# Seven-product feed-forward on one core: gate and up in turn, sums on VectorE, output weights two blocks at a time

## The chip, the cores and the metric

The kernel runs on one core of a Trainium2 chip. The metric is the device time of one execution in microseconds (us), the median of several runs. A core has TensorE (PE, the matrix engine, with PEld for its weight loads), VectorE (DVE), ScalarE (ACT), GpSimd (POOL) and SyncE (SP, which only issues transfers here). Each engine works through its own list of instructions in order and waits on semaphores for the others. Matrix products gather in PSUM; everything else lies in SBUF.

## The reference

Two trunk layers over 640 tokens (128 of context, 512 latent) of width 1024, with the same weights for both kinds of token. The part that matters here is the feed-forward stage, of which each layer has two:

```python
D_MODEL = 1024
D_FF = 2816
def swiglu(x, wg, wu, wd):
    return (jax.nn.silu(x @ wg) * (x @ wu)) @ wd
def trunk_layer(h, cond, p, ctx):
    ...
    x = rmsnorm(h, p["norm_ffn2"]) * (1 + sc3) + sh3
    h = h + 0.5 * g3 * swiglu(x, p["ffn2_w_gate"], p["ffn2_w_up"], p["ffn2_w_down"])
    return h, new_ctx
```

All of it is in float32. After the second layer only a last normalisation follows.

## The kernel before

**Numbers.** Every float32 operand of a product is held as a high and a low part (`whi`, `wlo` for weights, `xh`, `xl` for the input, `hh`, `hl` for the hidden activation), and a product is three matmuls: high by high, low by high, high by low. The high part is made on ACT (L232), the low part by a subtraction on DVE (L233).

**Tiling.** Activations stand with the model width on the partitions and tokens as columns, in two halves of 256 and 384 columns. The 2816 hidden columns are 22 f blocks of 128. A feed-forward stage goes through chunks of f blocks: the gate and up products of a chunk, SiLU and the product of the two (`hx`), its split into `hh` and `hl`, and then the output phase (`res_phase`), in which 8 output blocks of 128 are summed over the f blocks of the chunk and added to the residual `hT` by DVE (L679).

**The last feed-forward stage.** Only the second layer's second one (`l` 1, `j` 2) uses `CHUNKS_S`, and it is the place of the whole change. Its first chunk is computed plainly: the first two f blocks (the lead group, L754 to L764) by half, each half for both blocks with the inner dimension outermost, other f blocks one at a time through `mm3` (L309 to L311). From `CHUNKS_S[1][0]` on, f blocks go in pairs through `st_pair`, a scheme with 7 block products in place of 8 (Strassen's, in Winograd's form): weights and input are cut in two by two blocks, 128 f columns by 512 of the width, and 512 of the width by 320 tokens. For gate and for up in turn it runs the products named 11, 21, T2, T1, T3, 22 and T4, each 12 matmuls of 320 columns (L852 to L854). Between them ACT copies partial results out of PSUM (`cp`, L859), DVE adds them to the next (`sg`, L867, or `hx`, L874) and multiplies gate and up (L876). `a` and `c` are two halves of one PSUM tile, of which there are two.

**The sums.** T1, T2, T3 and T4 on the input side are sums of input blocks, made once in `st_x`, a generator that is stepped at L763 in the lead group and run out at L796, ahead of the first output phase. It uses DVE and POOL. On the weight side a slab of two f blocks (8 k blocks by 256 columns, 1 MB, tile `raw`) is used in four forms (`W_ST`): A1 as loaded, and S1, S3 and S24, which `st_sums` makes with four instructions on POOL, three of them in place.

**What sets the order.** `wq` lists the weight pieces in the order of use. `prep_to(n)` splits pieces up to number n into slots of a ring (five in this stage), and asks for the next slab (`load_upto`, issued on SP at L208) when one of the three `raw` buffers comes free; `w(ahead)` takes the next piece and prepares some ahead. An output slab holds two output blocks of 128 columns for the f blocks of the chunk, two pieces. The first two output blocks of a seven-product chunk take the f blocks of the first pair early (`early`), beside the second pair. On top of the order in which the code is written, the framework's scheduler arranges the instructions of each engine by a model of their times.

## Time and profile before

| | |
|---|---|
| median of 3 runs | 2614.9 us (2613.13 to 2615.86) |
| profiled execution | 2610.76 us |
| its span in the trace | 2609.0 us |
| PE busy | 2471.4 us, 95% |
| DVE busy | 1656.3 us, 63% |
| ACT busy | 904.7 us, 35% |
| POOL busy | 458.4 us, 18% |
| read from HBM | 254.44 MB |

The share of PE in the span is an average over stages that differ. The last feed-forward stage runs from about 2100 us to 2598 us of the span; what a change there is worth is read from the stretches of that stage: how long PE is busy in each, and which wait ends last. A matmul's own duration is longer than its distance to the next one, since matmuls overlap, so the floor of a stretch is made from distances between starts.

### The profile page before, as it was taken

How to read it: one execution, taken by the hardware profiler on the slowest of the kernel's cores; microseconds unless marked ns; L12 is line 12 of the kernel's file. 1: busy time of each engine (PE TensorE's matmuls, PEld its weight loads, DVE VectorE, ACT ScalarE, POOL GpSimd, SP SyncE). 2: the span in 40 equal slices, each digit the busy share in tenths (PEclk: the TensorE clock that was granted, in tenths of full speed). 3: DMA queues.
4: the chain of work that ended last, by engine and by line, in shares of the span. 5: the costliest groups of instructions: out<-in, count | busy, mean ns of one | idle time of the engine just before them, and what ended most of it. 6: DMA issues, size and time to landing. Idle time of an engine off the chain costs nothing.

```text
span 2609.0 us, 41506 instructions
## 1 busy us (share of the span) xinstructions
PE 2471.4 (95%) x16800; PEld 2314.1 (89%) x16800; DVE 1656.3 (63%) x3308; ACT 904.7 (35%) x1760; POOL 458.4 (18%) x553
## 2 busy tenths in 40 slices
PE   7999999999899999999999999999979968998898
PEld 5999999987679899999999999999756868898888
DVE  5767676665777776454366666656477785555455
ACT  5332222242544332222242122224245444333334
POOL 2210100036002121000011000003510052312220
PEclk8999999999999999999999999999989989999999
DMA  8545454330104345243125444432110211222121
GB/s 291 167 126 166 141 162 145 106 117 24 58 17 126 96 139 178 86 129 107 56 87 156 130 146 138 139 112 92 44 53 19 86 49 53 81 89 73 49 81 57
DMA packets 209223, 272.09 MB, mean 104 GB/s; under 512 B 25672, under 2 KB 176424, under 8 KB 208776
## 3 DMA queue, kind: packets, MB, share of 16 engines
q1 hardware_dynamic: 187016, 191.45, 23.3%
q0 software_dynamic: 22016, 78.00, 10.2%
q8 instruction: 132, 2.16, 0.3%
q14 instruction: 59, 0.48, 0.1%
HBM read 254.44 MB, written 14.97 MB: 103 GB/s over the span
## 4 chain that ended last, share of the span: by engine, by line
PE 82%; DVE 8%; ACT 3%; POOL 3%; DMA 2%; issue 1%; SPq 0%; DVEq 0%; ACTq 0%; POOLq 0%
PE gu L309 11%; PE gu L311 11%; PE gu L310 11%; PE y L309 9%; PE y L310 8%; PE y L311 8%; PE st L852 3%; PE st L853 3%; PE st L854 2%; ACT whi L232 2%; PE O L1771 1%; PE y L1869 1%; DVE wlo L233 1%; PE gu L761 1%; PE gu L759 1%; PE gu L760 1%
## 5 line engine op out<-in xcount | busy, mean ns | idle before, releaser
L232 ACT ACTIVATE whi<-raw 128x1024 fp32r<-128x1024 f32 (+3 forms) x388 | 353.4, 918 | 792.4 <-PE y L310 332.7
L233 DVE TENSOR_TENSOR wlo<-raw,whi 128x1024 fp32r<-128x1024 f32 (+3 forms) x388 | 419.2, 1084 | 293.1 <-ACT whi L232 291.6
L309 PE MATMUL gu<-xh,whi 128*128 128x384 f32 (+1 forms) x1920 | 595.6, 310 | 0.8 <-ACT whi L232 0.8
L310 PE MATMUL gu<-xl,whi 128*128 128x256 f32 (+1 forms) x1920 | 591.5, 308 | 0.0
L311 PE MATMUL gu<-xh,wlo 128*128 128x256 f32 (+1 forms) x1920 | 591.2, 308 | 0.3 <-DVE wlo L233 0.3
L309 PE MATMUL y<-hh,whi 128*128 128x384 f32 (+1 forms) x1328 | 413.9, 313 | 17.7 <-ACT hh L775 17.7
L310 PE MATMUL y<-hl,whi 128*128 128x384 f32 (+1 forms) x1328 | 410.7, 310 | 0.0
L311 PE MATMUL y<-hh,wlo 128*128 128x384 f32 (+1 forms) x1328 | 410.5, 310 | 0.0
L309 PEld LDWEIGHTS gu<-xh,whi 128*128 128x128 f32 x1920 | 360.2, 188 | 11.7 <-issue 10.0
L310 PEld LDWEIGHTS gu<-xl,whi 128*128 128x128 f32 x1920 | 360.9, 188 | 2.6 <-issue 2.4
L311 PEld LDWEIGHTS gu<-xh,wlo 128*128 128x128 f32 x1920 | 360.4, 188 | 1.3 <-issue 0.8
L679 DVE SCALAR_TENSOR_TENSOR hT<-y,G,hT 128x128 f32<-128x128 f32 (+1 forms) x504 | 203.5, 434 | 166.3 <-PE y L311 161.9
L444 DVE SCALAR_TENSOR_TENSOR mvec<-wm,cs,mvec 128x512 f32<-128x512 f32 x420 | 294.3, 744 | 9.9 <-DMA wm<-in_w_mod_dram 9.6
L309 PEld LDWEIGHTS y<-hh,whi 128*128 128x128 f32 x1328 | 252.3, 191 | 25.3 <-ACT hh L775 17.9
L399 POOL DMA_DIRECT2D wm<-in_w_mod_dram x128 | 92.4, 722 | 1037.3 <-DVE mvec L444 794.0
L310 PEld LDWEIGHTS y<-hl,whi 128*128 128x128 f32 x1328 | 252.7, 190 | 0.1
L311 PEld LDWEIGHTS y<-hh,wlo 128*128 128x128 f32 x1328 | 252.5, 190 | 0.4 <-issue 0.4
L852 PE MATMUL st<-xh,whi 128*128 128x320 f32 x320 | 100.7, 316 | 20.1 <-DVE hx L874 8.8
L774 DVE TENSOR_TENSOR hx<-sg,gu 128x256 f32<-128x256 f32 (+1 forms) x136 | 65.5, 482 | 82.4 <-ACT sg L772 82.1
L775 ACT ACTIVATE hh<-hx 128x256 fp32r<-128x256 f32 (+1 forms) x136 | 64.0, 471 | 137.1 <-DVE hx L774 136.8
L772 ACT ACTIVATE sg<-gu 128x256 f32<-128x256 f32 (+1 forms) x136 | 58.2, 430 | 139.3 <-PE gu L311 136.5
L776 DVE TENSOR_TENSOR hl<-hx,hh 128x256 fp32r<-128x256 f32 (+1 forms) x136 | 70.1, 518 | 44.9 <-ACT hh L775 44.8
(392 smaller groups left out, 4404.7 us busy)
## 6 DMA issues: line engine op xcount, KB each, us to landing
wm<-in_w_mod_dram POOLq DMA_DIRECT2D x128, 512.0 KB, 4.2
raw<-in_ffn_w_gate_dram SPq DMA_DIRECT2D x44, 1024.0 KB, 5.4
raw<-in_ffn_w_up_dram SPq DMA_DIRECT2D x44, 1024.0 KB
raw<-in_ffn_w_down_dram SPq DMA_DIRECT2D x36, 512.0 KB, 3.7
raw<-in_ffn_w_down_dram SPq DMA_DIRECT2D x16, 1024.0 KB, 7.5
raw<-in_w_in_dram SPq DMA_DIRECT2D x12, 1024.0 KB, 6.0
raw<-in_ffn_w_down_dram SPq DMA_DIRECT2D x12, 768.0 KB, 5.3
wf<-in_w_mod_dram SPq DMA_DIRECT2D x8, 1024.0 KB, 12.6
```

What stands on the lines that cost most here:

```text
L232: self.nc.scalar.activation(hv, v, AF.Copy)
L233: self.nc.vector.tensor_tensor(lv, v, hv, op=OP.subtract)
L309: self.nc.tensor.matmul(out, wh, xh, start=(i == 0), stop=False)
L310: self.nc.tensor.matmul(out, wh, xl, start=False, stop=False)
L311: self.nc.tensor.matmul(out, wl, xh, start=False, stop=(i == n - 1))
L399: self.nc.gpsimd.dma_start(out=t.rearrange("p (j c) -> p j c", j=2), in_=w[kk * 256:(kk + 1) * 256, c0:c0 + 512].rearrange("(j p) c -> p j ...
L444: nc.vector.scalar_tensor_tensor(self.mvec[:, v], w, c, self.mvec[:, v], op0=OP.mult, op1=OP.add)
L679: self.pin = nc.vector.scalar_tensor_tensor(h, y[:, s:e], G[:, k, v:v + 1], h, op0=OP.mult, op1=OP.add)
L774: nc.vector.tensor_tensor(hx[:, 0:w], sg[:, 0:w], u, op=OP.mult)
L776: self.pin = nc.vector.tensor_tensor(hl[half][:, f, :], hx[:, 0:w], hh[half][:, f, :], op=OP.subtract)
L852: nc.tensor.matmul(o, h, bh[:, k, :], start=start and k == 0, stop=False, skip_group_check=True)
L853: nc.tensor.matmul(o, h, bl[:, k, :], start=False, stop=False, skip_group_check=True)
```

## The change

All of it lies in the last feed-forward stage.

1. `CHUNKS_S` begins with (0, 4), (4, 2) in place of (0, 2), (2, 4): the plain chunk has four f blocks, the first seven-product chunk one pair. There are nine pairs in all, ten before.
2. `st_sums` runs on DVE, and when S1 is split, not when A1 is. `W_ST` becomes A1, S1, S24, S3, and `wq` takes gate and up by turns within each kind. S1's split has tiles of its own, outside the ring.
3. `st_x` runs its sums on DVE alone and makes T1's source a second time in place of keeping it: 60 instructions on DVE, where there were 28 on DVE and 20 on POOL. It is stepped after each product of the plain single f blocks, not in the lead group.
4. `st_pair` runs each of the seven products for gate and then for up, where it ran all seven for gate and then all seven for up. Of the `sg` tiles there are three, not four.
5. Output weights are split two blocks at a time: one piece of 256 columns (`w_down` hands out its halves), and all output blocks of this stage go two at a time. The last `FIN_S` = 6 blocks, 5 before, are run half by half.

```diff
-CHUNKS_S = ((0, 2), (2, 4), (6, 4), (10, 4), (14, 4), (18, 4))
+CHUNKS_S = ((0, 4), (4, 2), (6, 4), (10, 4), (14, 4), (18, 4))
...
-S1_BUFS = 1
-W_ST = ("A1", "S24", "S1", "S3")
+FIN_S = 6
+W_ST = ("A1", "S1", "S24", "S3")
...
+            if f == "S1":
+                hi = self.sx.tile([P, 512], F32R, tag="s1h", name="whi", bufs=2)
+                lo = self.sx.tile([P, 512], F32R, tag="s1l", name="wlo", bufs=2)
+            else:
+                sl = self.i_ring % self.ring_n
+                self.i_ring += 1
+                pool = self.ring_a if sl < RING_A else self.ring_b
+                hi = pool.tile([P, 1024], F32R, tag=f"h{sl}", name="whi")
+                lo = pool.tile([P, 1024], F32R, tag=f"l{sl}", name="wlo")
...
-            if f == "A1":
-                self.st_sums(sid, raw)
...
         if f == "S1":
-            return self.s1.pop(sid)
+            return self.st_sums(raw)
...
-        G = self.nc.gpsimd
+        G = self.nc.vector
...
-        s1 = self.sx.tile([P, 4, P], F32, name="s1", tag="s1", bufs=S1_BUFS)
+        s1 = self.t(512, "s1")[:, 0:512].rearrange("p (k n) -> p k n", k=4)
...
-                            self.add_slab(slab(w, f, 2), W_ST)
+                            self.add_slab(slab(w, f, 2), ())
+                            self.slab_left[len(self.slabs) - 1] = len(W_ST)
+                            if key == "u":
+                                self.wq += [(len(self.slabs) - 2 + i, kind) for kind in W_ST for i in range(2)]
...
-                self.add_slab((src, [P, n, 256]), [(lambda v: v[:, :, 0:P]), (lambda v: v[:, :, P:2 * P])])
+                if st < FB:
+                    self.add_slab((src, [P, n, 256]), [lambda v: v])
+                else:
+                    self.add_slab((src, [P, n, 256]), [(lambda v: v[:, :, 0:P]), (lambda v: v[:, :, P:2 * P])])
...
+    def w_down(self, pairs, ahead):
+
+        if not pairs:
+            return [self.w(ahead)]
+        w = self.w(ahead)
+        return [tuple(v[:, :, i * P:i * P + P] for v in w) for i in range(2)]
...
-                        if half == 1 and k % 2:
-                            next(tprep, None)
...
                         self.mm3(outs[s], [(wh[:, k, :], wl[:, k, :], xh[:, k, :], xl[:, k, :]) for k in range(DB)])
+                        next(tprep, None)
...
-            r12, r11, r22 = whole(V, k, TH), whole(V, k, 0), whole(G, 4 + k, TH)
-            t1 = self.sx.tile([P, TH], F32, name="sg", tag="sg", bufs=4)
-            t1s.append(t1)
-            V.tensor_tensor(t1, r12, r11, op=OP.subtract)
-            G.tensor_tensor(r12, r22, r12, op=OP.subtract)
-            split(G, r12, *(t[:, k, TH:NTOK] for t in self.T23))
-            V.tensor_tensor(r22, r22, t1, op=OP.subtract)
-            split(V, r22, *(t[:, k, 0:TH] for t in self.T23))
-            r21 = whole(G, 4 + k, 0)
-            G.tensor_tensor(r21, r21, r22, op=OP.subtract)
-            split(V, r21, *(t[:, k, :] for t in self.T4))
+            r12, r11, r22 = whole(k, TH), whole(k, 0), whole(4 + k, TH)
+            V.tensor_tensor(r11, r12, r11, op=OP.subtract)
+            V.tensor_tensor(r12, r22, r12, op=OP.subtract)
+            split(r12, *(t[:, k, TH:NTOK] for t in self.T23))
+            yield
+            r21 = whole(4 + k, 0)
+            V.tensor_tensor(r22, r22, r11, op=OP.subtract)
+            V.tensor_tensor(r21, r21, r22, op=OP.subtract)
+            split(r22, *(t[:, k, 0:TH] for t in self.T23))
+            split(r21, *(t[:, k, :] for t in self.T4))
             yield
         for k in range(4):
-            split(V, t1s[k], *(t[:, k, TH:NTOK] for t in self.xt))
+            r12, r11 = whole(k, TH), whole(k, 0)
+            V.tensor_tensor(r12, r12, r11, op=OP.subtract)
+            split(r12, *(t[:, k, TH:NTOK] for t in self.xt))
...
-            g = sg[i, t] = self.sx.tile([P, TH], F32, name="sg", tag="sg", bufs=4)
+            g = sg[i, t] = self.sx.tile([P, TH], F32, name="sg", tag="sg", bufs=3)
...
-        for done in (gate, up):
-            ac = self.d2("st")
-            a, c = ac[:, 0, 0:TH], ac[:, 1, 0:TH]
-            b = self.b([P, 512], name="st")[:, 0:TH]
-            w1 = self.w(2)
-            prod(a, w1, 0, "11", True)
-            t1 = copy(a)
-            prod(b, w1, 4, "21", True)
-            done(0, 0, b, t1)
-            w2 = self.w(2)
-            prod(a, w2, 0, "T2", False)
-            u2 = copy(a)
-            w4 = self.w(2)
-            prod(c, w4, 0, "T1", True)
-            t5 = copy(c)
-            w3 = self.w(2)
-            prod(a, w3, 0, "T3", False)
-            done(1, 1, a, t5)
-            prod(c, w2, 4, "22", False)
-            done(0, 1, c, u2)
-            prod(a, w3, 4, "T4", False)
-            done(1, 0, a, None)
+        B = range(2)
+        done = (gate, up)
+        ac = [self.d2("st") for _ in B]
+        a, c = ([t[:, i, 0:TH] for t in ac] for i in range(2))
+        b = [self.b([P, 512], name="st")[:, 0:TH] for _ in B]
+
+        def pair(o, w, k0, x, start, then):
+            out = []
+            for u in B:
+                prod(o[u], w[u], k0, x, start)
+                out.append(then(u))
+            return out
+
+        w1 = [self.w(2) for _ in B]
+        t1 = pair(a, w1, 0, "11", True, lambda u: copy(a[u]))
+        pair(b, w1, 4, "21", True, lambda u: done[u](0, 0, b[u], t1[u]))
+        w4 = [self.w(1) for _ in B]
+        w2 = [self.w(1) for _ in B]
+        u2 = pair(a, w2, 0, "T2", False, lambda u: copy(a[u]))
+        t5 = pair(c, w4, 0, "T1", True, lambda u: copy(c[u]))
+        w3 = [self.w(0) for _ in B]
+        pair(a, w3, 0, "T3", False, lambda u: done[u](1, 1, a[u], t5[u]))
+        pair(c, w2, 4, "22", False, lambda u: done[u](0, 1, c[u], u2[u]))
+        self.prep_to(self.i_use + 2)
+        pair(a, w3, 4, "T4", False, lambda u: done[u](1, 0, a[u], None))
...
-        first = DB if nxt is None else DB - FIN
+        fin = FIN_S if pairs else FIN
+        first = DB if nxt is None else DB - fin
...
-            wds = [self.w(self.ahead) for _ in range(k)]
+            k = 2 if pairs else lead if db == 0 else 1
+            wds = []
+            while len(wds) < k:
+                wds += self.w_down(pairs, self.ahead)
...
+            one(DB - fin + db, h0, wds[db])
+            self.prep_to(self.i_use + min(db, 1 if pairs else self.ring_n - FIN))
```

The change moves instructions. First VectorE at the end of the first chunk's gate and up. Before, these rows stand ahead of `hx` of f blocks 0 and 1 (L774; `tr`, `t23l` and `t4l` are tiles of `st_x`):

```order
L822 TENSOR_TENSOR t23l_20675<-tr_20768,t23h_20674 128x320 [waits Activation_49]
L831 TENSOR_TENSOR tr_20811<-tr_20811,sg_20813 128x320 [waits Pool_49]
L822 TENSOR_TENSOR t4l_20677<-tr_20778,t4h_20676 128x320 [waits Activation_49]
L822 TENSOR_TENSOR t23l_20675<-tr_20811,t23h_20674 128x320 [waits Activation_49]
L774 TENSOR_TENSOR hx_20828<-sg_20826,gu_20648 128x384 [waits DVE_49,Activation_49]
L774 TENSOR_TENSOR hx_20834<-sg_20832,gu_20649 128x384 [waits DVE_49,Activation_49]
L776 TENSOR_TENSOR hl_20454<-hx_20828,hh_20453 128x384 [waits Activation_49]
L776 TENSOR_TENSOR hl_20454<-hx_20834,hh_20453 128x384 [waits Activation_49]
```

After, the same place (`hx_20750` and `hx_20756` are those of f blocks 0 and 1; `hx` is L787 now, `wlo` L236, the sums of `st_x` L829 and L838):

```order
L787 TENSOR_TENSOR hx_20750<-sg_20748,gu_20650 128x384 [waits Activation_49]
L236 TENSOR_TENSOR wlo_20761<-raw_20459,whi_20760 128x1024 [waits Activation_49]
L236 TENSOR_TENSOR wlo_20765<-raw_20465,whi_20764 128x1024 [waits Activation_49]
L236 TENSOR_TENSOR wlo_20919<-raw_20642,whi_20918 128x1024 [waits DMAHW7_49,Activation_49]
L787 TENSOR_TENSOR hx_20756<-sg_20754,gu_20651 128x384 [waits DVE_49,PE_49,Activation_49]
L829 TENSOR_TENSOR tr_20797<-xh_20345,xl_20346 128x320 [waits DVE_49]
L829 TENSOR_TENSOR tr_20799<-xh_20345,xl_20346 128x320 [waits DVE_49]
L789 TENSOR_TENSOR hl_20454<-hx_20750,hh_20453 128x384 [waits Activation_49]
L829 TENSOR_TENSOR tr_20801<-xh_20345,xl_20346 128x320 [waits DVE_49,Pool_49]
L789 TENSOR_TENSOR hl_20454<-hx_20756,hh_20453 128x384 [waits Activation_49]
L838 TENSOR_TENSOR tr_20799<-tr_20797,tr_20799 128x320 [waits DVE_49]
```

The sums of `st_x` stood ahead of the two `hx`; now three weight splits stand between the two, and the sums follow behind both.

Second, PE near the end of a pair, where product 22 ends and T4 begins, in one PSUM tile. Before, for up (`st_21949`):

```order
L853 MATMUL st_21949<-xl_20346,whi_21901 128x320
L854 MATMUL st_21949<-xh_20345,wlo_21902 128x320
L852 MATMUL st_21949<-xh_20345,whi_21901 128x320
L853 MATMUL st_21949<-xl_20346,whi_21901 128x320
L854 MATMUL st_21949<-xh_20345,wlo_21902 128x320
L852 MATMUL st_21949<-t4h_20676,whi_21986 128x320 [waits DVE_49]
L853 MATMUL st_21949<-t4l_20677,whi_21986 128x320
L854 MATMUL st_21949<-t4h_20676,wlo_21987 128x320
L852 MATMUL st_21949<-t4h_20676,whi_21986 128x320
```

After, for both (`st_22044` is gate, `st_22045` up):

```order
L867 MATMUL st_22045<-xh_20345,wlo_22131 128x320
L865 MATMUL st_22045<-xh_20345,whi_22130 128x320
L866 MATMUL st_22045<-xl_20346,whi_22130 128x320
L867 MATMUL st_22045<-xh_20345,wlo_22131 128x320
L865 MATMUL st_22044<-t4h_20795,whi_22134 128x320 [waits DVE_49]
L866 MATMUL st_22044<-t4l_20796,whi_22134 128x320
L867 MATMUL st_22044<-t4h_20795,wlo_22135 128x320
L865 MATMUL st_22044<-t4h_20795,whi_22134 128x320
L866 MATMUL st_22044<-t4l_20796,whi_22134 128x320
```

T4 followed 22 of the same tile, and T3 stood right ahead of them; now between T3 and T4 of one tile lie three products, one of its own and two of the other.

Third, VectorE at the second pair of a chunk, from the end of the first pair. Before (`raw_21885` is a slab of the second pair, `raw_22013` an output slab):

```order
L876 TENSOR_TENSOR hx_22079<-st_21949,sg_21947 128x320 [waits PE_49]
L233 TENSOR_TENSOR wlo_22137<-raw_21885,whi_22136 128x1024 [waits DMAHW4_49,Activation_49]
L867 TENSOR_TENSOR sg_22115<-st_22084,cp_22101 128x320 [waits Activation_49]
L879 TENSOR_TENSOR hl_21822<-hx_22079,hh_21821 128x320 [waits Activation_49]
L233 TENSOR_TENSOR wlo_22162<-raw_21885,whi_22161 128x1024 [waits Activation_49]
L233 TENSOR_TENSOR wlo_22285<-raw_22013,whi_22284 128x512 [waits DVE_49,DMAHW5_49,PE_49,Activation_49]
L233 TENSOR_TENSOR wlo_22247<-raw_21885,whi_22246 128x1024 [waits PE_49,Activation_49]
L874 TENSOR_TENSOR hx_22241<-st_22210,cp_22227 128x320 [waits DVE_49,Activation_49]
L876 TENSOR_TENSOR hx_22241<-hx_22241,sg_22115 128x320 [waits DVE_49]
L867 TENSOR_TENSOR sg_22177<-st_22083,cp_22159 128x320 [waits PE_49]
L879 TENSOR_TENSOR hl_21822<-hx_22241,hh_21821 128x320 [waits Activation_49]
```

After (`raw_22436` and `raw_22500` are gate's and up's slab of the second pair, `raw_22784` an output slab):

```order
L880 TENSOR_TENSOR sg_22884<-st_22824,cp_22856 128x320 [waits Activation_49]
L236 TENSOR_TENSOR wlo_22841<-s1_22835,whi_22840 128x512 [waits Activation_49]
L259 TENSOR_TENSOR raw_22436<-s1_22826,raw_22436 128x4x128 [waits DVE_49]
L259 TENSOR_TENSOR raw_22500<-s1_22835,raw_22500 128x4x128 [waits DVE_49]
L236 TENSOR_TENSOR wlo_22913<-raw_22436,whi_22912 128x1024 [waits Activation_49]
L236 TENSOR_TENSOR wlo_23041<-raw_22784,whi_23040 128x1024 [waits DMAHW5_49,PE_49,Activation_49]
L887 TENSOR_TENSOR hx_22899<-st_22825,cp_22870 128x320 [waits Activation_49]
L260 TENSOR_TENSOR raw_22436<-raw_22436 128x4x128 [waits DVE_49]
L236 TENSOR_TENSOR wlo_22973<-raw_22500,whi_22972 128x1024 [waits Activation_49]
L260 TENSOR_TENSOR raw_22500<-raw_22500 128x4x128 [waits DVE_49]
L889 TENSOR_TENSOR hx_22899<-hx_22899,sg_22884 128x320 [waits DVE_49,Activation_49]
L236 TENSOR_TENSOR wlo_22905<-raw_22436,whi_22904 128x1024 [waits Activation_49]
```

VectorE had splits and the results of products there; the sums of both slabs (L257 to L260) now stand between them, and the split of an output slab ahead of S24's.

## Rows read from the trace of the kernel before

**Rows 1.** Table by stretches: stretch, length, busy us (instructions) of PE, PEld, DVE, ACT, POOL; clock, DMA share, GB/s

```profile
2099.00:2106.00 7.00, 4.27 (x15) 3.90 (x15) 6.35 (x9) 5.00 (x10) 3.51 (x3) 0.76 0.00 0
2121.00:2139.40 18.40, 0.74 (x8) 0.54 (x6) 18.00 (x26) 6.87 (x17) 13.57 (x15) 0.64 0.23 71
...
2165.00:2253.60 88.60, 80.56 (x530) 77.36 (x529) 48.26 (x77) 31.58 (x52) 22.61 (x16) 1.00 0.23 72
...
2430.70:2519.30 88.60, 80.46 (x529) 77.33 (x528) 49.00 (x76) 31.58 (x52) 22.34 (x16) 1.00 0.23 72
```

**Rows 2.** Timeline of DVE and PE: start, length, engine, line, operation, out<-in, idle before and releaser

```profile
2122.63 1.15 DVE L831 TENSOR_TENSOR tr<-tr,sg 128x320 f32<-128x320 f32 x1
...
2139.40 0.90 PE L309 MATMUL y<-hh,whi 128*128 128x384 f32 x2 [17.66 <-ACT hh L775]
```

**Rows 3.** Waits of PE, 2150 to 2575: waiting line, awaited, us, times, longest

```profile
PE st L852 <- DVE hx L874: 14.7, 20, 1.5
PE st L852 <- ACT cp L859: 13.4, 10, 1.4
PE st L852 <- ACT whi L232: 5.8, 10, 0.6
PE st L852 <- DVE hx L876: 5.5, 5, 1.1
```

**Rows 4.** Timeline of PE: first and last matmul of three runs, and the last output matmul

```profile
2239.77 0.28 PE L311 MATMUL y<-hh,wlo 128*128 128x256 f32 x1
...
2240.84 0.28 PE L311 MATMUL y<-hh,wlo 128*128 128x256 f32 x1
2240.96 0.34 PE L309 MATMUL y<-hh,whi 128*128 128x384 f32 x1
...
2242.88 0.33 PE L311 MATMUL y<-hh,wlo 128*128 128x384 f32 x1
2243.05 0.30 PE L852 MATMUL st<-xh,whi 128*128 128x320 f32 x1
...
2245.98 0.31 PE L854 MATMUL st<-xh,wlo 128*128 128x320 f32 x1
...
2597.82 0.28 PE L311 MATMUL y<-hh,wlo 128*128 128x256 f32 x1
```

**Rows 5.** Timeline of DVE in a seven-product chunk

```profile
2197.69 1.23 DVE L233 TENSOR_TENSOR wlo<-raw,whi 128x1024 fp32r<-128x1024 f32 x1 [0.69 <-ACT whi L232]
2198.84 0.48 DVE L874 TENSOR_TENSOR hx<-st,cp 128x320 f32<-128x320 f32 x1
2199.36 0.49 DVE L876 TENSOR_TENSOR hx<-hx,sg 128x320 f32<-128x320 f32 x1
2200.10 0.49 DVE L867 TENSOR_TENSOR sg<-st,cp 128x320 f32<-128x320 f32 x1 [0.25 <-PE st L854]
2200.51 0.48 DVE L879 TENSOR_TENSOR hl<-hx,hh 128x320 fp32r<-128x320 f32 x1
...
2222.69 0.68 DVE L233 TENSOR_TENSOR wlo<-raw,whi 128x512 fp32r<-128x512 f32 x1
2223.29 0.61 DVE L679 SCALAR_TENSOR_TENSOR hT<-y,G,hT 128x384 f32<-128x384 f32 x1
```

**Rows 6.** Groups by line and shape, 2150 to 2575: busy us, mean ns, idle before

```profile
L233 DVE TENSOR_TENSOR wlo<-raw,whi 128x1024 fp32r<-128x1024 f32 x60 | 82.2, 1369 | 76.4 <-ACT whi L232 76.2
L232 ACT ACTIVATE whi<-raw 128x1024 fp32r<-128x1024 f32 x59 | 62.5, 1060 | 111.5 <-POOL raw L259 44.5 <-PE y L310 33.5 <-PE st L853 32.9
```

**Rows 7.** Timeline of PE around the lead group's second half

```profile
2100.93 0.45 PE L759 MATMUL gu<-xh,whi 128*128 128x384 f32 x1 [1.88 <-ACT xh L639]
...
2102.40 0.69 PE L761 MATMUL gu<-xl,whi 128*128 128x384 f32 x1 [0.85 <-DVE xl L640]
...
2120.70 0.34 PE L761 MATMUL gu<-xl,whi 128*128 128x384 f32 x1
```

**Rows 8.** Page's part on DMA issues: KB each, median us from issue to landing

```profile
raw<-in_ffn_w_gate_dram SPq DMA_DIRECT2D x44, 1024.0 KB, 5.4
```

More of the change, by code (lines that the diff above doesn't have):

```diff
@@ L217, in prep_to @@
             if f in W_ST:
-                v = self.st_view(sid, raw, f)
+                v = self.st_view(raw, f)
             else:
@@ L221, in prep_to @@
             k, w = v.shape[1], v.shape[2]
-            sl = self.i_ring % self.ring_n
-            self.i_ring += 1
-            pool = self.ring_a if sl < RING_A else self.ring_b
-            hi = pool.tile([P, 1024], F32R, tag=f"h{sl}", name="whi")
-            lo = pool.tile([P, 1024], F32R, tag=f"l{sl}", name="wlo")
+            if f == "S1":
[7 more added lines that the diff above has]
+                lo = pool.tile([P, 1024], F32R, tag=f"l{sl}", name="wlo")
             hv = hi[:, 0:k * w].rearrange("p (k n) -> p k n", k=k)
@@ L241, in prep_to, with st_view, st_sums @@
             self.i_prep += 1
[L243 removed]
+    def st_view(self, raw, f):
         if f == "S1":
[L246 removed]
+            return self.st_sums(raw)
         return raw[:, :, P:2 * P] if f == "S3" else raw[:, :, 0:P]
[L249 to L252 removed]
+    def st_sums(self, raw):
+        G = self.nc.vector
         a11, a12 = raw[:, 0:4, 0:P], raw[:, 4:8, 0:P]
         a21, a22 = raw[:, 0:4, P:2 * P], raw[:, 4:8, P:2 * P]
[L255 removed]
+        s1 = self.t(512, "s1")[:, 0:512].rearrange("p (k n) -> p k n", k=4)
         G.tensor_tensor(s1, a21, a22, op=OP.add)
@@ L799, in ffn @@
             self.res_phase(n, [(hh[i], hl[i]) for i in range(2)], [(f, f) for f in range(n)], (l, j), nxt if last else None,
-                           early=(n - 2 if c0 >= st else 0))
+                           early=(n - 2 if c0 >= st else 0), pairs=st < FB)
         if st < FB:
@@ L1840, in out1, with res_phase @@
                 yield
-    def res_phase(self, n, xs, order, G, nxt, lead=1, early=0):
+    def res_phase(self, n, xs, order, G, nxt, lead=1, early=0, pairs=False):
         nc = self.nc
@@ L1859, in res_phase @@
         if early:
-            wds = [self.w(1) for _ in range(2)]
+            wds = self.w_down(pairs, 1)
             ys = [(i, half, self.b([P, 512], name="y")) for i in range(2) for half in range(2)]
@@ L1885, in res_phase @@
             return
-        wds = [self.w(0) for _ in range(FIN)]
+        wds = []
+        while len(wds) < fin:
+            wds += self.w_down(pairs, 0)
         h0, h1 = (1, 0) if nxt[1] is None else (0, 1)
-        for db in range(FIN):
-            one(DB - FIN + db, h0, wds[db])
-            self.prep_to(self.i_use + min(db, self.ring_n - FIN))
+        for db in range(fin):
+            one(DB - fin + db, h0, wds[db])
+            self.prep_to(self.i_use + min(db, 1 if pairs else self.ring_n - FIN))
         self.x = [None, None]
@@ L1893, in res_phase @@
         self.fine = True
-        for db in range(FIN):
-            one(DB - FIN + db, h1, wds[db])
+        for db in range(fin):
+            one(DB - fin + db, h1, wds[db])
         self.fine = False
```

17 lines of the change are left out of this document (6 added, 11 removed).

## The prediction

> **What bounds the kernel now.** The profiled execution took 2610.76 us (span 2609.0 and 1.76 around it), 4.1 under the median of 2614.9, so what the sum saves is taken off the median. The order of work is unchanged until 2098, where the last feed-forward stage begins, so everything below lies there. TensorE (PE) is the limit whenever it is fed, and I read first what it waits for. The table by stretches shows PE busy 0.74 of 18.40 us up to 2139.4, at a granted clock of 0.64 [rows 1]. The wait itself: one product of the output phase stands 17.66 us for a hidden activation `hh` [rows 2]. The four full chunks repeat every 88.6 us [rows 1]. The waits of PE there are on a copy out of PSUM, on `hx` and on weight splits, and sum to 39.4 us over five chunks [rows 3], about 8 a chunk.
>
> Pitches make the floor. Nine starts of 256-column matmuls take 1.07 us (0.119 each), eleven of 384 take 1.92 (0.1745), twenty of 320 take 2.93 (0.1465) [rows 4]. One product of 12 is 1.76 us. A pair of f blocks in seven products (168 matmuls) is 24.6, in the plain form 96 x (0.119 + 0.1745) = 28.2, and the output phase costs 24 x 0.2935 = 7.04 per f block. A chunk of two pairs is 49.2 + 28.2 = 77.4, so 11.2 of 88.6 are lost: about 8 in ten waits, and some 0.3 per wait to get going again. From 2121, where the stretch of the long wait begins [rows 1], to the last output product (2597.8, [rows 4]) are 477 us, of which 10 x 24.6 + 22 x 7.04 = 401 are floor.
>
> **One pair fewer in seven products.** Nine instead of ten: +28.2 - 24.6 = +3.6 us.
>
> **The end of the 17.66 us wait.** Before, 28 instructions of `st_x` on VectorE (DVE) and 20 on GpSimd (POOL) lie ahead of the two `hx` that PE waits for. DVE is busy 18.00 of 18.40 us in that stretch, POOL 13.57 [rows 1], and an instruction of 320 columns that takes 0.48 in the chunks [rows 5] takes 1.15 here [rows 2]. After, 60 such instructions run on DVE with POOL idle, spread over the plain f blocks 2 and 3. Their pitch is 0.41 where the next needs nothing and 0.52 where it does [rows 5]; I take 0.45.
>
> The long splits on DVE, which lie beside GpSimd's sums in the chunks, take 1.37 on average and 1.23 where GpSimd is still; the short sums beside GpSimd's share of `st_x` took 1.15 against 0.48 [rows 2, 5, 6]. So the rows show a loss of a tenth in one place and of a half in the other, and it is the second, with POOL idle after, that 0.45 rests on. The Trainium skill (SBUF: State Buffer, Who interferes with whom) states that a VectorE instruction with two inputs in SBUF and a GpSimd instruction that reads SBUF take turns at a shared port, each for its whole length. By that rule the 60 sums cost the same 60 x 0.45 = 27 us once GpSimd is idle, and 60 x 1.15 = 69 if they had to share; by the rows alone the two numbers are the same.
>
> Start of the stage: PE stands 1.88 and then 0.85 us for `xh` and `xl` [rows 7], and the clock of that stretch is 0.76 [rows 1]. In the new order the first 24 matmuls of f block 2 (2.8 us) lie in this gap. The group still starts when `xl` is there, 2102.4, but at full clock. A clock of 0.76 over 7 us is some 3 us at half of it, ten matmuls of 384 columns, each about 0.15 us dearer than its pitch; so the group ends 1.5 earlier than 2120.9, where its last matmul hands over before [rows 7]: at 2119.4. Then a new wait: the up weights of f block 2 need a ring slot that this group holds, so 1.06 on ScalarE (ACT) and 1.23 on DVE follow [rows 5, 6], with the restart 2.7 us. The rest of blocks 2 and 3 is 25.4: the output phase begins at 2147.5. On DVE four long splits x 1.15, two products of 384 columns x 0.61 and 1.06 on ACT ahead of them end 6.9 after 2119.4 [rows 5, 6]; then 61 short instructions (47 of `st_x`) x 0.45 and four splits x 1.15 = 32, so the last `hl` of the chunk is there at 2158.3. PE has 80 matmuls (11.7 us) ahead of it in the order, to 2159.2. I charge 1 us. The phase ends at 2147.5 + 28.2 + 1 = 2176.7. The T1 parts and the sums for the first pair (21 us of DVE) fit behind that phase and the two double products before T2.
>
> **Gate and up in turn.** Each copy, `sg` and `hx` now has 1.76 us or more of the other product over it, against 0.4 to 0.5 an instruction. The waits on `cp` (13.4) and `hx` (14.7 + 5.5) [rows 3] go. What is late next is the weights.
>
> **Sums on DVE.** Eight of 512 columns per pair at 0.60 [rows 5], 4.8 us; by the duration, 0.68, it would be 5.4. Per pair DVE has 6 splits x 1.15 + 2 x 0.60 + 4.8 + 14 short x 0.45 = 19.2 of PE's 24.6. Enough on average; the queue decides. For a chunk's first pair the weights are made under the output phase before, and nothing waits. For the second pair the order puts the sums behind the last `hx` of the first. Count from the end of T4 of up, t = 0, on DVE: mult 0.5, two sums 1.7, `hl` 2.1, two sums 3.3, S1 3.9, `sg` 4.3, S1 4.9, two sums 6.1, S3 7.3, output weights 8.4, `hx` 8.8, sum 9.4, S3 10.6, sum 11.2, mult 11.6, S24 of gate 12.8, of up 14.0. PE has 11 of both (3.5), then 6 early output matmuls that need ACT's `whi` at 4.95, 20 more that need the 8.5 above, then T2, whose `whi` of up is there at 12.4: waits of 1.4, 2.7 and 0.9, in all 5.0, with restarts 5.9. Four chunks have such a pair: 23.6 us. Of this, 1.15 each is the output split, now 1024 columns (ACT 1.06) in place of 512, that stands ahead of S24; elsewhere that edit is hidden under the output phase.
>
> **Loads.** SP issues the next pair's gate slab once the second output slab is split, 3 us before t = 0 of the second pair, and a slab of 1 MB lands 5.4 us after its issue [rows 8], so at 2.4. `s1` waits for it at the head of DVE's queue, with the last `hl` behind it, and so does ACT's `whi`. For PE about 2.3 us and restarts, 3.4, at three chunk ends, 2.6 at the short chunk, 1.6 at the last. Fewer `sg` buffers and the six last output blocks cost nothing that a row shows; the 11 us behind the last product stay.
>
> **Sum.** 2176.7; short chunk 24.6 + 14.1 + 2.6 = 41.3, to 2218.0; four chunks 4 x 77.4 = 309.6 and 23.6 + 10.2 + 1.6 = 35.4, to 2563.0. Before it was 2597.9: 34.9 us less. On the median 2614.9 - 34.9 = 2580.0.
>
> **Rivals.**
> A, DVE is not late. If the second pair's weights come in time, 23.6 us more go: 2556. For it: DVE is far from full in a chunk, 48 of 88.6 us [rows 1]. Against: the sums stand behind `hx` in an in-order queue. Chance 0.17.
>
> B, the waits are dearer. Gaps of 1.88 and 0.85 us are followed by a clock of 0.76 over that stretch [rows 1, 7], where ten matmuls cost 1.5 us more (as above); eight such places give 12, and sums at 0.68 add 0.6 to each second pair: 2594. Chance 0.23. The Trainium skill (Perfetto Trace Analysis, Optimizing Scalar/DVE Operations) warns that moving work between GpSimd and VectorE might not help; no row of before has the sums on VectorE alone.
>
> C, slower: the loads become the bound. Two of three slab buffers are held by gate and up until S3 and S24 are split. If every pair waits for a full landing and split, 5.4 + 1.06 + 1.23 = 7.7 [rows 5, 6, 8], nine pairs cost 69: 2649. The side turns at 34.9 / 9 = 3.9 us per pair. Against: the second pair's up slab is asked for when S3 of gate is split, ten us before its first use. Chance 0.06.
>
> D, the order is new but the gain is eaten elsewhere, within 0.2%: 0.04.
>
> **How the numbers follow.** The forecast has 0.50. Its own spread is about 8 us. The range takes in A and B and leaves out C, D and the outer tails: 2553 to 2602. A measurement here tells 0.2% (5 us) from no change. Faster 0.90, same 0.04, slower 0.06.
>
> **What would show it.** After: no wait over 3 us in the output phase of the first chunk, and full clock there. Chunks of 84 to 87 us with waits on `wlo` and `whi` at the early output products and T2 of the second pair, none on `cp`. DVE's short instructions at 0.48 throughout, POOL idle. Chunks of 80 would mean A, matmuls at half pitch behind the gaps B, waits on `raw` of several us in every pair C. A first output phase that still stands for `hh` would make the forecast wrong.

## The result and the profile after

The changed kernel takes 2579.16 us in the median of four runs (2577.18 to 2583.58); the kernel before took 2614.98 beside it. The ratio is 0.9866, with a 95% interval of 0.9849 to 0.9883. The profiled execution took 2577.18 us, its span is 2575.4. The part ahead of the last feed-forward stage takes the same instructions in all but the same order in every kernel here, and yet it ends anywhere from 2097.8 to 2107.7 us in their profiled executions; so stages are compared within a trace, and whole kernels by medians.

The page after, first the busy times:

```profile
PE 2466.1 (96%) x16824; PEld 2316.6 (90%) x16824; DVE 1662.7 (65%) x3378; ACT 893.1 (35%) x1726; POOL 324.5 (13%) x453
...
HBM read 254.44 MB, written 14.97 MB: 105 GB/s over the span
```

VectorE's share hardly moved: it took over GpSimd's sums, and its instructions are no longer stretched by GpSimd. The table by stretches after (stretch, length, busy us of PE, PEld, DVE, ACT, POOL, clock, DMA share, GB/s), to be read against [rows 1]:

```profile
2099.00:2106.00 7.00, 6.61 (x42) 5.57 (x41) 6.14 (x9) 4.76 (x10) 3.29 (x3) 1.00 0.00 0
2121.00:2146.50 25.50, 24.97 (x166) 24.97 (x167) 24.17 (x48) 12.82 (x23) 0.00 (x0) 1.00 0.48 152
2146.50:2220.80 74.30, 73.38 (x494) 72.07 (x493) 61.76 (x127) 26.43 (x44) 0.00 (x0) 1.00 0.18 55
2248.76:2335.11 86.35, 80.70 (x528) 78.89 (x528) 52.41 (x89) 30.61 (x49) 0.00 (x0) 0.98 0.23 74
2335.11:2423.34 88.23, 81.89 (x528) 80.09 (x528) 52.51 (x89) 30.61 (x49) 0.00 (x0) 0.96 0.23 72
2423.34:2509.45 86.11, 80.59 (x528) 78.81 (x529) 52.32 (x89) 30.60 (x49) 0.00 (x0) 0.98 0.23 74
2509.45:2565.50 56.05, 52.74 (x342) 51.65 (x342) 36.42 (x72) 24.26 (x45) 1.14 (x1) 0.94 0.11 38
```

The first three rows are the gain: where PE stood 17.66 us at a clock of 0.64, it is now busy in 25 of 25.5 and in 73.4 of 74.3 us, at full clock, while VectorE alone carries the sums (24.17 of 25.50 busy) and POOL does nothing. The full chunks, three of which run from early wait to early wait here, take 86.1 to 88.2 us, against 88.6 before: little was won there, and the clock is no longer 1.00. The waits of PE from 2095 to 2570 say why (awaited, us in total, times, longest):

```profile
PE y L1886 <- DVE wlo L236: 10.2, 4, 2.6
PE y L1886 <- ACT whi L235: 5.5, 4, 1.4
PE st L865 <- ACT whi L235: 3.1, 5, 0.9
PE y L1886 <- DVE hl L892: 3.0, 4, 0.8
```

Nothing is left of the waits on `cp` and `hx` [rows 3]; the two large rows now are weight splits that come late, at the early output products (L1886), in each of the four second pairs. PE's timeline at one of them (start, length, line, operation, idle before):

```profile
2335.11 0.39 PE L1886 MATMUL y<-hh,whi 128*128 128x256 f32 x1 [1.38 <-ACT whi L235]
...
2335.93 0.28 PE L1886 MATMUL y<-hl,whi 128*128 128x256 f32 x1
2338.76 0.58 PE L1886 MATMUL y<-hh,wlo 128*128 128x256 f32 x1 [2.55 <-DVE wlo L236]
...
2343.20 0.52 PE L1886 MATMUL y<-hl,whi 128*128 128x384 f32 x1
2343.51 0.52 PE L1886 MATMUL y<-hh,wlo 128*128 128x384 f32 x1
...
2345.25 0.31 PE L865 MATMUL st<-t23h,whi 128*128 128x320 f32 x1
2345.40 0.31 PE L866 MATMUL st<-t23l,whi 128*128 128x320 f32 x1
```

PE idles 1.38 us, runs six matmuls, idles 2.55 us, and what follows starts every 0.31 us for 384 columns, near twice the 0.1745 of [rows 4]: the lower of the two clock levels, 1.2 GHz, until about 2344.9. The same two waits stand in all four second pairs, and the clocks of the table (0.98, 0.96, 0.98, 0.94) come to some 3.4, 7, 3.4 and 6.7 us at 1.2 GHz behind them. VectorE's timeline just ahead of it:

```profile
2330.33 0.49 DVE L889 TENSOR_TENSOR hx<-st,sg 128x320 f32<-128x320 f32 x1 [2.90 <-PE st L867]
2330.74 1.28 DVE L257 TENSOR_TENSOR s<-raw 128x512 f32<-128x512 f32 x2
2331.94 0.48 DVE L892 TENSOR_TENSOR hl<-hx,hh 128x320 fp32r<-128x320 f32 x1
...
2335.15 1.29 DVE L259 TENSOR_TENSOR raw<-s,raw 128x512 f32<-128x512 f32 x2
2336.35 2.35 DVE L236 TENSOR_TENSOR wlo<-raw,whi 128x1024 fp32r<-128x1024 f32 x2
```

VectorE stands idle for 2.90 us until PE ends T4 of up, and only then begins the sums for the next pair, which stand behind that `hx` in its queue. The second half of the last row is the output split that PE awaits at 2338.76.

### The profile page after: what moved, and what is told of

It is laid out like the page before. It is cut to its first block, busy times and chain, and to the rows that moved or that the text cites. A ratio compares the mean times of both kernels' runs of the same rounds, so it can differ in the third digit from the quotient of the medians.

```text
span 2575.4 us, 41416 instructions
## 1 busy us (share of the span) xinstructions
PE 2466.1 (96%) x16824; PEld 2316.6 (90%) x16824; DVE 1662.7 (65%) x3378; ACT 893.1 (35%) x1726; POOL 324.5 (13%) x453
## 3 DMA queue, kind: packets, MB, share of 16 engines
q0 software_dynamic: 22016, 78.00, 10.3%
## 4 chain that ended last, share of the span: by engine, by line
PE 83%; DVE 9%; DMA 3%; POOL 2%; ACT 2%; issue 1%; SPq 0%; DVEq 0%; ACTq 0%; POOLq 0%
PE gu L310 11%; PE gu L312 11%; PE gu L311 11%; PE y L310 9%; PE y L311 8%; PE y L312 8%; PE st L865 2%; PE st L866 2%; PE st L867 2%; DVE wlo L236 1%; PE O L1787 1%; PE gu L775 1%; PE gu L773 1%; PE gu L774 1%; PE pj L1227 1%; PE y L1886 1%
## 5 line engine op out<-in xcount | busy, mean ns | idle before, releaser
L310 PE MATMUL gu<-xh,whi 128*128 128x256 f32 (+1 forms) x1984 | 616.0, 310 | 0.8 <-ACT whi L235 0.8
L312 PE MATMUL gu<-xh,wlo 128*128 128x256 f32 (+1 forms) x1984 | 611.3, 308 | 0.9 <-DVE wlo L236 0.9
L311 PE MATMUL gu<-xl,whi 128*128 128x256 f32 (+1 forms) x1984 | 611.5, 308 | 0.0
L235 ACT ACTIVATE whi<-raw 128x1024 fp32r<-128x1024 f32 (+2 forms) x362 | 347.0, 964 | 757.8 <-PE y L311 340.1
L236 DVE TENSOR_TENSOR wlo<-raw,whi 128x1024 fp32r<-128x1024 f32 (+2 forms) x362 | 399.1, 1107 | 218.1 <-ACT whi L235 215.1
L310 PE MATMUL y<-hh,whi 128*128 128x256 f32 (+1 forms) x1344 | 417.0, 312 | 0.4 <-DVE hT L680 0.3
L311 PE MATMUL y<-hl,whi 128*128 128x256 f32 (+1 forms) x1344 | 414.7, 309 | 0.6 <-DVE hl L892 0.6
L312 PE MATMUL y<-hh,wlo 128*128 128x256 f32 (+1 forms) x1344 | 414.6, 309 | 0.0
L310 PEld LDWEIGHTS gu<-xh,whi 128*128 128x128 f32 x1984 | 372.5, 188 | 11.9 <-issue 10.0
L311 PEld LDWEIGHTS gu<-xl,whi 128*128 128x128 f32 x1984 | 373.2, 188 | 2.7 <-issue 2.4
L787 DVE TENSOR_TENSOR hx<-sg,gu 128x256 f32<-128x256 f32 (+1 forms) x140 | 67.7, 484 | 81.2 <-ACT sg L785 81.1
L595 POOL TENSOR_TENSOR rst<-ms,mhalf 128x2 f32<-128x2 f32 (+1 forms) x12 | 11.5, 956 | 836.2 <-DVE ms L594 836.2
```

Source lines behind the costliest of these rows:

```text
L235: self.nc.scalar.activation(hv, v, AF.Copy)
L236: self.nc.vector.tensor_tensor(lv, v, hv, op=OP.subtract)
L310: self.nc.tensor.matmul(out, wh, xh, start=(i == 0), stop=False)
L311: self.nc.tensor.matmul(out, wh, xl, start=False, stop=False)
L312: self.nc.tensor.matmul(out, wl, xh, start=False, stop=(i == n - 1))
L787: nc.vector.tensor_tensor(hx[:, 0:w], sg[:, 0:w], u, op=OP.mult)
```

## The experiments

All start from the changed kernel and change what their diff shows. Medians are of four runs each, beside seven of the kernel before on the same chip (2614.9 to 2615.4). The table gives the full chunks that were read from each trace: length, PE's waits in one of them and the clock. Not tried apart from the rest are the pair count, the six last output blocks, the three `sg` tiles and the new order of the four forms.

| kernel | median us | ratio to before, 95% | a full chunk | waits of PE in it | clock |
|---|---|---|---|---|---|
| before | 2615.0 | | 88.6 | 7.9 (39.4 / 5) | 1.00 |
| changed | 2579.2 | 0.9849 to 0.9883 | 86.1 to 88.2 | 6.4 in the longest | 0.96 to 0.98 |
| e1_serial | 2595.6 | 0.9911 to 0.9940 | 89.2 | 7.7 | 1.00 |
| e2_pool_sums | 2574.0 | 0.9827 to 0.9860 | 83.2 to 85.7 | 4.4 | 0.96 to 1.00 |
| e3_stx_pool | 2584.8 | 0.9867 to 0.9907 | 86.4 | 5.8 | 0.98 |
| e4_single_out | 2578.0 | 0.9837 to 0.9870 | 85.5 to 85.9 | 4.5 | 0.96 |
| e5_first_two | 2604.6 | 0.9940 to 0.9973 | 86.4 | 5.8 | 0.98 |
| e6_early4 | 2567.6 | 0.9802 to 0.9836 | 82.7 to 82.8 | 3.1 | 1.00 |
| e8_early22 | 2576.2 | 0.9834 to 0.9863 | 85.4 | 5.1 | 0.98 |
| e10_early4_single | 2557.5 | 0.9759 to 0.9790 | 80.1 to 80.2 | 1.6 | 1.00 |
| e12_early4_single_pool | 2566.7 | 0.9801 to 0.9831 | 82.7 | 4.2 | 1.00 |
| e13_early5_single | 2558.0 | 0.9769 to 0.9802 | 80.1 | 1.5 | 1.00 |
| e14_no_sums | 2561.0 | 0.9780 to 0.9809 | 82.0 | 2.4 | 0.98 |

### Undoing one part at a time

**e1_serial** undoes the alternation of gate and up, in the products and in the order of the weight pieces.

```diff
-        w1 = [self.w(2) for _ in B]
-        t1 = pair(a, w1, 0, "11", True, lambda u: copy(a[u]))
...
+        for done in (gate, up):
+            w1 = self.w(2)
+            prod(a, w1, 0, "11", True)
+            t1 = copy(a)
...
```

> The changed kernel with one part undone: a pair runs all seven products for gate and then all seven for up, as before, and the weight pieces are queued slab by slab; sums on VectorE, chunks and output weights stay new. Theory (the alternation hides the copies and hx): waits of TensorE on cp and hx come back, some 7 us a chunk of two pairs and half that in the short one, in all 4.5 x 7 = 32, less what the waits on late weights in the second pair (5.4 a chunk) ease because the weights of up are needed later: 2590 to 2612. Rival (the weights are the limit either way, so the alternation hides nothing that would show): 2575 to 2586.

Measured: 2595.6, 16.4 above the changed kernel. The theory holds. Waits of PE in two chunks of e1_serial:

```profile
PE st L862 <- DVE sg L877: 6.1, 8, 1.0
PE st L862 <- DVE hx L884: 4.8, 8, 0.7
PE st L862 <- ACT cp L869: 4.4, 8, 0.6
```

They are the waits of before, on copies and on their sums, 7.7 us a chunk, and the early waits on weights are gone. Note the clock: these 24 waits of up to 1 us leave it at 1.00, while fewer and longer ones in the changed kernel do not.

**e5_first_two** gives the first chunk two plain blocks again.

```diff
-CHUNKS_S = ((0, 4), (4, 2), (6, 4), (10, 4), (14, 4), (18, 4))
+CHUNKS_S = ((0, 2), (2, 4), (6, 4), (10, 4), (14, 4), (18, 4))
...
+                        if half == 1 and k % 2:
+                            next(tprep, None)
+                            next(tprep, None)
```

> The changed kernel with the first chunk back at two plain f blocks, ten pairs in seven products, and the x sums stepped in the lead group again (all 60 on VectorE). Theory (the two plain blocks are the cover for the x sums): 60 x 0.45 = 27 us of VectorE and the splits behind it face 20 us of the lead group, so TensorE waits for hh some 8 to 15 us again and runs at half clock behind that, less 3.6 for the pair that is again in seven products: 2583 to 2598. Rival (the sums on VectorE alone are quick enough without cover): 2573 to 2578.

Measured: 2604.6, 25.5 above the changed kernel and 6.6 above the top of what was expected. A wait of 12.46 us is back, in the expected size; it stands at a product of the first pair, on `t4h` of the x sums, and not at the output phase (timeline of PE, then the stretches around it):

```profile
2140.15 0.60 PE L868 MATMUL st<-xh,whi 128*128 128x320 f32 x1 [12.46 <-ACT t4h L836]
```

```profile
2126.00:2140.15 14.15, 1.70 (x14) 1.52 (x13) 13.61 (x32) 6.76 (x15) 0.00 (x0) 0.73 0.68 221
2140.15:2150.00 9.85, 9.85 (x47) 9.85 (x48) 9.85 (x26) 4.08 (x8) 0.00 (x0) 0.69 0.02 4
```

VectorE is busy in 13.61 of 14.15 us with POOL idle: one engine without cover still leaves PE idle for 12.46 us, where two that hinder each other left it idle for 17.66. The expectation left out two things. The chunk (2, 4) then has a second pair of its own, the fifth, with the waits and the clock of such a pair; and PE's waits of 1.88 and 0.85 us at the start of the stage [rows 7] are back too, since no matmuls of f block 2 fill them. So the 25.5 us are the price of all of this together, and not of the place of the sums alone.

**e3_stx_pool** shares the x sums with GpSimd in the new place.

```diff
-            r12, r11, r22 = whole(k, TH), whole(k, 0), whole(4 + k, TH)
-            V.tensor_tensor(r11, r12, r11, op=OP.subtract)
-            V.tensor_tensor(r12, r22, r12, op=OP.subtract)
+            r12, r11, r22 = whole(V, k, TH), whole(V, k, 0), whole(G, 4 + k, TH)
+            V.tensor_tensor(r11, r12, r11, op=OP.subtract)
+            G.tensor_tensor(r12, r22, r12, op=OP.subtract)
...
```

> The changed kernel with the x sums shared between the engines as before (40 on VectorE, 20 on GpSimd), in the new places beside the plain f blocks 2 and 3. Theory (both the engine and the cover matter, the cover more): the 40 on VectorE go from 0.45 to about 1.15 beside GpSimd, 46 us against 27, so the last hl of the first chunk comes some 15 us later and the first output phase or the first pair waits 3 to 12 us: 2582 to 2594. Rival 1 (the place alone did it, the engine is free to choose): 2576 to 2582. Rival 2 (one engine alone was the mistake, sharing helps here): under 2575.

Measured: 2584.8, 5.6 above the changed kernel, the lower part of the theory's range. One group of the x sums on VectorE (busy us, mean ns), in the kernel before from 2121 to 2139.4, then from 2121 to 2160 in e3_stx_pool and in the changed kernel:

```profile
L817 DVE TENSOR_TENSOR tr<-xh,xl 128x320 f32<-128x320 f32 x4 | 3.3, 818 | 0.0
```

```profile
L829 DVE TENSOR_TENSOR tr<-xh,xl 128x320 f32<-128x320 f32 x12 | 9.1, 788 | 0.0
```

```profile
L829 DVE TENSOR_TENSOR tr<-xh,xl 128x320 f32<-128x320 f32 x22 | 10.4, 488 | 0.0
```

Fewer sums on VectorE take nearly as long, 788 ns each against 488. PE then waits 2.13 us for `hl` in the first output phase and 1.28 for `whi` in the first pair. So the engine is worth some 5 us here; the slowest run of the changed kernel (2583.6) is still above the fastest of this one (2581.7), and it is the two waits in the trace that bear the reading out.

**e2_pool_sums** puts the weight sums back on GpSimd.

```diff
-        G = self.nc.vector
+        G = self.nc.gpsimd
```

> The changed kernel with the weight sums back on GpSimd, all else new. Theory (the second pair waits because its sums stand in VectorE's queue behind the last hx): the sums can start earlier but take 1.3 to 1.6 each on GpSimd, eight in a row some 12 us against 11.6 on VectorE after the same point, and the long splits on VectorE go back from 1.23 to about 1.37: 2572 to 2592, and the waits move from the early output products to T2. Rival 1 (VectorE's load alone made the weights late): 2555 to 2568. Rival 2 (the two engines hinder each other so much that sums on GpSimd cost more in all): over 2595.

Measured: 2574.0, 5.2 *below* the changed kernel. That is in the theory's range, but the shift of the waits that went with it did not come: they stay at the early output products, 1.05 and 1.90 in place of 1.38 and 2.55. GpSimd's four kinds of sum take 1.44 to 1.75 us each on average, and the splits of S1 beside them on VectorE go from 683 ns to 1402 (2200 to 2550, the changed kernel first):

```profile
L236 DVE TENSOR_TENSOR wlo<-s,whi 128x512 fp32r<-128x512 f32 x16 | 10.9, 683 | 0.0
```

```profile
L236 DVE TENSOR_TENSOR wlo<-s,whi 128x512 fp32r<-128x512 f32 x16 | 22.4, 1402 | 0.0
```

What stands in VectorE's queue at the start of the second pair is 4.8 us shorter, though (eight sums at 0.60), and that would outweigh it. In the order of the changed kernel this part of the change costs time: some 5 us by the medians, whose two intervals overlap a little, and chunks of 83.2 to 85.7 us against 86.1 to 88.2 in the traces.

**e4_single_out** splits output weights one block at a time.

```diff
-                if st < FB:
-                    self.add_slab((src, [P, n, 256]), [lambda v: v])
-                else:
-                    self.add_slab((src, [P, n, 256]), [(lambda v: v[:, :, 0:P]), (lambda v: v[:, :, P:2 * P])])
+                self.add_slab((src, [P, n, 256]), [(lambda v: v[:, :, 0:P]), (lambda v: v[:, :, P:2 * P])])
```

> The changed kernel with output weights split one block at a time again, as before the change. Theory (the wide output split stands ahead of S24 and before the early products): ACT's split of 0.63 instead of 1.06 and VectorE's of 0.68 instead of 1.23 come sooner by about half a microsecond each, so the first early wait falls from 1.38 to about 0.9 and the second from 2.55 to about 2, but the second block's split then stands in the same queue: 2574 to 2580. Rival 1 (wide splits save time because there are fewer): 2582 to 2592. Rival 2 (the wide split is what makes the second pair late): 2560 to 2572.

Measured: 2578.0, within the runs of the changed kernel, as the theory had it. The first early wait falls to 0.96; the second stays at 2.7, since the second block's split stands in the queue too. The waits of 0.76 on `hl` at the chunk's end are gone, and one of 0.83 on `whi` at T2 of the second pair is new.

### Moving the sums

**e6_early4** changes one number.

```diff
-        self.prep_to(self.i_use + 2)
+        self.prep_to(self.i_use + 4)
         pair(a, w3, 4, "T4", False, lambda u: done[u](1, 0, a[u], None))
```

> The changed kernel with one number changed: before T4 of a pair four weight pieces are prepared ahead, not two, so that the next pair's S1 and the sums are in the program ahead of T4 and its hx. Theory (the sums stand behind the last hx while VectorE idles 2.9 us for T4): the sums start some 3.4 us earlier, the waits of 1.38 and 2.55 at the early output products and that of T2 go for the most part, and with them the half clock behind: 4 to 8 us in each of four chunks, 2547 to 2565. Rival 1 (the slab's landing and A1's split set the time, not the order): 2574 to 2583. Rival 2 (the sums now delay hx and so T4 or the output): over 2584.

Measured: 2567.6, 11.5 below the changed kernel, a little above the theory's range. VectorE at the same place, with the sums in the former gap and the `hx` of T4 among them:

```profile
2327.66 1.28 DVE L257 TENSOR_TENSOR s<-raw 128x512 f32<-128x512 f32 x2
2328.87 0.48 DVE L889 TENSOR_TENSOR hx<-hx,sg 128x320 f32<-128x320 f32 x1
2329.27 1.29 DVE L258 TENSOR_TENSOR raw<-raw 128x512 f32<-128x512 f32 x2
...
2332.68 0.68 DVE L259 TENSOR_TENSOR raw<-s,raw 128x512 f32<-128x512 f32 x1
2333.28 0.48 DVE L889 TENSOR_TENSOR hx<-st,sg 128x320 f32<-128x320 f32 x1
```

The 2.55 us wait is gone, the longest is 0.77, and all chunks run at full clock:

```profile
2337.56:2420.28 82.72, 79.68 (x529) 77.38 (x529) 52.28 (x90) 30.12 (x49) 0.00 (x0) 1.00 0.24 77
```

VectorE has the same work as in the changed kernel (52.3 us busy a chunk). So what these 11.5 us hung on was the place in the queue, not the load.

**e14_no_sums** prices the sums: they are left out, and S1, S24 and S3 are split straight from the slab.

```diff
-        s1 = self.t(512, "s1")[:, 0:512].rearrange("p (k n) -> p k n", k=4)
-        G.tensor_tensor(s1, a21, a22, op=OP.add)
-        G.tensor_tensor(a21, a11, a21, op=OP.subtract)
-        G.tensor_tensor(a11, s1, a11, op=OP.subtract)
-        G.tensor_tensor(a12, a12, a11, op=OP.subtract)
-        return s1
+        return a21
```

> The changed kernel without the weight sums: S1, S24 and S3 are split straight from the slab, so the weight products use other numbers; every split, product and transfer stays. It prices the sums. Theory (the sums in VectorE's queue are what makes the second pair late): the waits of 1.38 and 2.55 go and the half clock behind them, 4 to 8 us in each of four chunks and some in the first pair: 2545 to 2563. Rival (splits and landings alone are late too): 2568 to 2580.

Measured: 2561.0, 18.2 below the changed kernel and in the theory's range. In that order the sums cost 18 us. The waits in the second pairs are gone; what stays is at three chunk ends, where the first product of the next chunk waits 1.3 to 1.5 us on ScalarE's `whi`.

**e10_early4_single** joins e6_early4 and e4_single_out.

> As e6_early4, and with output weights one block at a time. Theory (with the sums early, half a microsecond of output split ahead of S24 is the rest of the wait): 2562 to 2567. Rival (wide splits pay once the sums are out of the way): 2569 to 2580.

Measured: 2557.5, 10.2 below e6_early4 and 4.5 under the theory's range, which had half a microsecond a chunk. It is the fastest here, 2.25% under the kernel before and 3.5 us under the kernel without sums. One chunk, and the waits of PE in it:

```profile
2256.26:2336.46 80.20, 78.66 (x529) 77.21 (x528) 52.34 (x93) 31.54 (x53) 0.00 (x0) 1.00 0.25 79
```

```profile
PE st L863 <- ACT whi L235: 1.2, 2, 0.8
PE st L865 <- DVE wlo L236: 0.4, 1, 0.4
```

Besides the early products' wait on `whi`, the 0.75 us on `hl` at the end of each chunk goes, which comes with the wide splits (it is in the changed kernel and e6_early4, and not in e4_single_out). In the changed kernel the next gate slab's `s` stands ahead of the last `hl` in VectorE's queue, and VectorE stands 1.29 us for its landing:

```profile
2365.30 0.69 DVE L257 TENSOR_TENSOR s<-raw 128x512 f32<-128x512 f32 x1 [1.29 <-DMA raw<-in_ffn_w_gate_dram]
2365.91 0.48 DVE L892 TENSOR_TENSOR hl<-hx,hh 128x320 fp32r<-128x320 f32 x1
```

With single blocks that `s` comes behind the last `hl` (2360.28 and 2362.80 in e10_early4_single), where PE waits for no `hl`. That the wide splits give the output slabs back sooner, and so bring the gate slab forward, would explain the two orders; it was not tried by itself.

**e13_early5_single** takes the fifth piece ahead too (`+ 5` in place of `+ 4`).

> As e10_early4_single, with a fifth piece (S24 of gate) prepared ahead of T4. Theory (the last waits, 0.5 each, are on S24 split on ScalarE late in its queue): 2552 to 2557. Rival (S24 can't be split before the sums are through, so nothing moves): 2556 to 2560.

Measured: 2558.0, with the same chunk of 80.1. The rival holds: nothing moves.

**e12_early4_single_pool** is e10_early4_single with the sums on GpSimd.

> As e10_early4_single, with the weight sums on GpSimd. Theory (the order of the sums is what counts; once they are early the engine matters little, and GpSimd's slower sums weigh against VectorE's lighter queue as in e2_pool_sums): 2551 to 2562. Rival 1 (sums of 1.5 on GpSimd make S24 late again): 2564 to 2576. Rival 2 (VectorE's load still counts): under 2550.

Measured: 2566.7, 9.2 above e10_early4_single: the first rival's range, and a miss of the theory. PE waits 1.5 us on `hx`, 1.2 and 0.9 on `wlo` in a chunk. So in these two orders GpSimd is the better engine for the sums while they are late (e2_pool_sums) and VectorE once they are early.

**e8_early22** moves the four pieces of e6_early4 ahead of product 22.

```diff
+        self.prep_to(self.i_use + 4)
         pair(c, w2, 4, "22", False, lambda u: done[u](0, 1, c[u], u2[u]))
-        self.prep_to(self.i_use + 2)
```

> As e6_early4, but the four pieces are prepared already ahead of product 22, one double product (3.5 us) earlier in the program. Theory (in e6_early4 the last waits of the second pair are on splits that the sums made late): the rest of them, 0.77 + 0.39 + 0.18 in each of four chunks, goes: 2560 to 2566. Rival (VectorE waits for the landing of up's slab, with hx behind it, since that slab is asked for only when S3 of gate is split): 2568 to 2580.

Measured: 2576.2, 8.6 above e6_early4. The number is the rival's, its reason is not what the waits show. PE waits on `cp` (5.3 in all) and `sg` (2.3) now, which ScalarE makes, beside 8.2 on `whi`, while VectorE stands no more than 1.0 us for any landing. PE at T2 of one second pair, and ScalarE just ahead of it:

```profile
2340.44 0.41 PE L865 MATMUL st<-t23h,whi 128*128 128x320 f32 x1 [1.33 <-ACT cp L872]
```

```profile
2339.00 1.06 ACT L235 ACTIVATE whi<-raw 128x1024 fp32r<-128x1024 f32 x1 [0.81 <-PE st L866]
2339.96 0.42 ACT L872 ACTIVATE cp<-st 128x320 f32<-128x320 f32 x1
```

The copy stands in ScalarE's queue behind a weight split that itself waits for a matmul of PE, 0.81 us here, and PE waits for the copy. ScalarE's waits of this kind (`whi` on PE, L866) are 23.9 us from 2230 to 2540, against 4.9 in the changed kernel. Why `sg` is late was not followed further. Too early is nearly as dear as too late.

## Why the prediction was right

The forecast was 2580.0 and the median came to 2579.2; the saving was 34.9 against 35.8, and 33.6 between the spans. The parts, in the order of the prediction:

- **The end of the 17.66 us wait.** Right. The stage's start ran at full clock (6.61 us busy of 7.00). The new weight wait after the lead group was 0.61 us and not the 2.7 with restart that were charged; against that the group ended about 1.1 later than 2119.4, with waits of 0.2, 0.2 and 0.5 for `xl` in it. The output phase began at 2146.5 (2147.5 forecast). The charged 1 us of waiting in it was 0.3. By 2220.8 PE had done 494 matmuls; the first output phase, one pair and the short chunk's output are 192 + 168 + 96 = 456, so 38 x 0.1465 = 5.6 of it belong to the next chunk, and the three were through at 2215.2, where 2218.0 was forecast. Of the 2.8 us, 1.0 is the earlier start; most of the rest is the load wait at the short chunk's end, charged with 2.6, which was 0.57 for `hl`, behind an `s` that stood 0.84 for its slab. The price of 1.15 for a sum of 320 columns beside GpSimd was read from one of the dearest rows: the group under e3_stx_pool took 0.82 before and 0.79 there, so 69 us for 60 shared sums is too much.
- **Gate and up in turn.** Right, as e1_serial shows by taking it back: 7.7 us a chunk of waits on copies and their sums return.
- **Sums on VectorE.** The place, the order and the sizes were right: 1.4 and 2.7 forecast for the early products, 1.38 and 2.55 measured; the third (0.9 at T2) was not there, which fits a PE that came to T2 later at half clock. What was mis-sized is what follows a wait: 0.9 us of restarts were charged, and the clock fell. Taking the part of a stretch that its clock falls short of 1.00 by, the four rows of the chunks give 0.02 x 86.35 + 0.04 x 88.23 + 0.02 x 86.11 + 0.06 x 56.05 = 10.3 us.
- **Loads.** The place was right, the size somewhat large: 2.3 of waits at each of three chunk ends forecast (3.4 with restarts), 1.7, 2.4 and 1.6 measured, of which 0.76 for `hl` and up to 0.86 and 0.80 for `whi`; 0.75 at the last.
- **The sum of the four chunks** was 345.0 forecast and 350.1 measured (2215.2 to 2565.3, where 2563.0 was forecast). 309.6 is the floor, 22 are waits, some 10 the clock, and the rest, 8, is left for the restarts of 18 waits; this last split is worked out, not shown row by row.

So the number was closer than its terms, and that part is luck: the clock, which the forecast left to rival B, took 10 us, and what was charged and did not come gave most of it back: 0.9 at each of four T2, 2 at the short chunk's load, 1.5 in the other loads and 1 at the start. Of the rivals, B was right in its mechanism and near its price (12 us of clock), at four places and not eight; its other part did not come, since two sums take 1.20 us from start to start, 0.60 each (2330.74 and 2331.94). A did not happen, and its price of 23.6 was not measured by itself: e14_no_sums puts the sums at 18, e6_early4 shows that 11.5 us hung on their order, and e10_early4_single, where the weights of the second pair are nearly in time, comes to 2557.5 close to A's 2556, with the chunks of 80 that were A's sign. C did not show: PE had no wait over 0.9 us that traces to a landing. The Trainium skill (Perfetto Trace Analysis, Optimizing Scalar/DVE Operations) says that moving work between GpSimd and VectorE might not help, because they share a read port; the runs agree in part. With the weight sums on VectorE and not on GpSimd the kernel lost 5 us in one order (e2_pool_sums) and won 9 in another (e12_early4_single_pool), so which engine is better hung on where in the queue the sums stood.
